# Transposes of a hybrid encoder block, written in pairs between its products

## The chip, the cores and the metric

The kernel runs on one core of a Trainium2 chip. The metric is device time in microseconds (us) for one launch. TensorE (PE in the profile) does the matrix products and the transposes; its weight loads are listed as PEld. VectorE is DVE, ScalarE is ACT, GpSimd is POOL, and SyncE is SP, which here only issues the loads of weights.

## The reference

One block of an encoder on x of 256 tokens by 2048 channels, in float32:

```python
proj = h @ w_in[l]
q, k, v, r, af, ab, hy_u, gate_logits = jnp.split(proj, split_idx, axis=-1)
y_gla = _gla_branch(q, k, v, r, af, ab, ...)   # 4 heads, chunks of 64 tokens, both directions
y_hy = _hyena_branch(hy_u, ...)                # short convolution, then z = gate * (conv(z) + skip*z), twice
g = jax.nn.sigmoid(gate_logits...).reshape(B, L, N_BRANCH, D)
merged = g[:, :, 0, :] * (y_gla @ w_gla_o[l]) + g[:, :, 1, :] * (y_hy @ w_hy_o[l])
mix = merged @ w_out[l]
h = _layernorm(DEEPNORM_ALPHA * h + mix, ln1_g[l], ln1_b[l])
ff = jnp.square(jax.nn.relu(h @ w_ff1[l])) @ w_ff2[l]
h = _layernorm(DEEPNORM_ALPHA * h + ff, ln2_g[l], ln2_b[l])
```

In the first branch each head's result o (256 x 512) is scaled by the reciprocal root of its mean square, by a learned gain and by a gate, which gives y. In the second branch the long convolutions are done as products with Fourier matrices.

## The kernel before

All weights lie in blocks of 128 x 2048 in the order of their use. `fetch` loads a block and splits each half into a high and a low part (`whi`, by ACT, L83; `wlo`, by DVE, L84), and `next_block` hands one out. Activations are held the same way in two parts. A product of two such numbers is three passes (high x low, high x high, low x high).

There are two kinds of product groups. `channel_pair` makes 128 channels by 256 tokens at a time; its `channel_products` has 16 high products of 512 columns (L144) and 16 low ones of 256 columns (L148) for each block. `token_group` makes 256 tokens by 512 channels; its `token_products` runs over the 16 slices of the contraction (kt) and the two halves of the tokens (tb), three products of 512 columns each (L196 to L198), and accumulates each half in one PSUM bank over four blocks.

Side work is put among these groups by hand. `later(d, fn)` files a function that is due d blocks on. After every block, `pump` calls what is due, and `drain` calls all that is left. This sets the order in which the program is written. The order in which each engine's instructions finally stand is made by a planner, which may move an instruction against its neighbours where its data and its priority allow it. `tc.keep_in_program_order(ins)` pins an instruction behind the one written before it on the same engine.

The side work that the change touches, in order of time:

- The heads (`gla_gates`, `gla_scores`, `gla_out`, filed 0, 4 and 7 blocks after each head's start, heads 6 blocks apart). `gla_gates` has products `z` (L504), then on ACT the gate pieces `ga` and `gm` (L508, L509), Exp and Ln (L511, L512), on DVE the running sums `gb`, then on ACT the exponentials `e` (L524, L525, L530) of each direction. `gla_scores` has products `s` (L580) and splits their result into `sth` and `stl`. `gla_out` has 12 products `o` (L296 to L298), ACT's square `y<-o` with its sum (L604), the small steps of the root (`rq_t`, `rq_y`, `rs`), DVE's `y` (L606), and 8 transposes of y into two banks `yt` (L613), which are split into yT.
- The convolution in 8 chunks of 256 channels. `hy_v` and `hy_x1` transpose the short convolution's results by `to_tokens` (`vt`, `x1t`, L673, 4 transposes each). `hy_fwd`, `hy_mul` and `hy_inv` make the long convolution. The second `hy_inv` has products `yp`, ACT's copy `zg` (L742), 4 transposes into `yT` (L746), and a product with x2, which goes to DRAM as `yd` and is read back as `yr` after the g2 groups.
- `merged`: for each of 4 groups, 8 transposes of the merged result into `mt` (L805), split into mT.
- The output product `wo` on mT, the first layer norm and the MLP. The pools `hp` and `qp` are closed and `ep` is opened ahead of wo.

A transpose is a TensorE instruction with the data as the moving operand's partner and `ident` as the other, 128 x 128 to PSUM.

Of the kernel before, what the change touches and what calls it, by code (L numbers as in the profile page):

```python
# [41 lines left out]
def block_kernel(  # L42
# [95 lines left out]
    def channel_products(ps, act, half, kts, ts=FULL, opens=True):  # L138
        hi, lo = half
        at = [(kt, slice(kt % 8 * P, (kt % 8 + 1) * P)) for kt in kts]  # L140

        def high():
            for kt, js in at:
                MM(ps[:, :, ts], hi[:, js], act[:, kt, :, ts], start=(kt == 0 and opens), stop=(kt == KT - 1))  # L144

        def low():
            for kt, js in at:
                MM(ps[:, 0, ts], lo[:, js], act[:, kt, 0, ts], start=False, stop=False)  # L148

        for part in (high, low) if kts[0] == 0 else (low, high):  # L150
            part()
# [33 lines left out]
    def token_products(pss, act, blocks, tbs, b0):  # L185
        for b, parts in enumerate(blocks):
            for h in range(2):
                hi, lo = parts[h]
                for j in range(2):
                    kt = (b0 + b) * 4 + h * 2 + j  # L190
                    wh = hi[:, j * 512:(j + 1) * 512]
                    wl = lo[:, j * 512:(j + 1) * 512]
                    for tb in tbs:
                        sh = act[:, kt, 0, tb * P:(tb + 1) * P]
                        sl = act[:, kt, 1, tb * P:(tb + 1) * P]
                        MM(pss[tb], sh, wh, start=(kt == 0), stop=False)  # L196
                        MM(pss[tb], sh, wl, start=False, stop=False)  # L197
                        MM(pss[tb], sl, wh, start=False, stop=(kt == KT - 1))  # L198

    def token_group(act, name):  # L200
        pss = [psum_main(f"{name}_{tb}") for tb in range(NT)]
# [390 lines left out]
    def gla_out(h):  # L592
        def run():
# [3 lines left out]
            for ib in range(NT):  # L597
                po = psum_side(f"o{h}{ib}")
                for jb in range(NT):
# [5 lines left out]
                hst["root"] = rsqrt_eps(rs, ss, 1.0 / 512.0, gp, f"rq{h}{ib}")  # L605
                nc.vector.scalar_tensor_tensor(  # L606
                    y[:, ib, :], po, rs, g_sb[:, ib, h * 512:(h + 1) * 512], op0=ALU.mult, op1=ALU.mult)
            for k2 in range(2):
                pt = psum_side(f"yt{h}{k2}")
                for kk in range(2):  # L610
                    for ib in range(NT):
                        kt = 2 * k2 + kk
                        nc.tensor.transpose(  # L613
                            pt[:, kk * L + ib * P:kk * L + (ib + 1) * P],
                            y[:, ib, kt * P:(kt + 1) * P], ident)
# [53 lines left out]
    def to_tokens(src, name):  # L669
        pt = psum_side(name)  # L670
        for c in range(2):
            for tb in range(NT):
                nc.tensor.transpose(pt[:, tb * CW + c * P:tb * CW + (c + 1) * P], src[:, c, tb * P:(tb + 1) * P], ident)  # L673
        return pt.rearrange("p (a b) -> p a b", a=2)

    def z_tiles(name):
        return (hp.tile([P, NT, CW], F32R, tag="zh", bufs=2, name=f"zh{name}"),
# [1 line left out]

    def hy_v(c):  # L680
        def run():
            z = z_tiles(f"{c}0")
            split_hi_lo(z[0], z[1], to_tokens(cst.pop(("v", c)), f"vt{c}"))
            cst[("z", c, 0)] = z
        return run

    def hy_x1(c):
        def run():
            x1 = hp.tile([P, NT, CW], F32, tag="x1", name=f"x1_{c}")
            nc.scalar.copy(x1, to_tokens(cst.pop(("x1c", c)), f"x1t{c}"))  # L690
            cst[("x1", c)] = x1
        return run

    def hy_fwd(c, o):
# [32 lines left out]
    def hy_inv(c, o):  # L727
        def run():
# [11 lines left out]
            else:  # L740
                zf = hp.tile([P, NT, CW], F32, tag="zf", name=f"zg{c}")
                nc.scalar.copy(zf, py3)  # L742
                pt = psum_side(f"yT{c}")
                for cc in range(2):
                    for tb in range(NT):
                        nc.tensor.transpose(pt[:, cc * L + tb * P:cc * L + (tb + 1) * P], zf[:, tb, cc * P:(cc + 1) * P], ident)  # L746
                yo = hp.tile([P, 2, L], F32, tag="zf", name=f"yo{c}")
                nc.vector.tensor_tensor(yo, pt.rearrange("p (a b) -> p a b", a=2), cst.pop(("x2", c)), op=ALU.mult)
                yd = drp.tile([P, 2, L], F32, tag=f"yd{c}", name=f"yd{c}")
                nc.gpsimd.dma_start(yd, yo)  # L750
                yh_dram[c] = yd
        return run

    go_done = [0]
# [26 lines left out]
            gla_o_group()  # L781


    g2_sb = qp.tile([P, 4, NT, 512], F32, tag="G", name="g2_sb")
# [5 lines left out]
    yhT = act_tile(base, "yT", "yh")  # L790
    for c in range(NCH):
        yr = hp.tile([P, 2, L], F32, tag="cv", bufs=2, name=f"yr{c}")
        nc.gpsimd.dma_start(yr, yh_dram[c])
        split_hi_lo(yhT[:, 2 * c:2 * c + 2, 0], yhT[:, 2 * c:2 * c + 2, 1], yr)
    mT = act_tile(base, "xT", "mT")

    def merged(g):
        def run():
            mg = m_group(g)
            for k2 in range(2):  # L800
                pt = psum_side(f"mt{g}{k2}")
                for kk in range(2):
                    for tb in range(NT):
                        kt = 2 * k2 + kk
                        nc.tensor.transpose(  # L805
                            pt[:, kk * L + tb * P:kk * L + (tb + 1) * P],
                            mg[:, tb, kt * P:(kt + 1) * P], ident)
# [12 lines left out]
    drain()  # L820
    hstk.close()
    qkg.close()


    ep = ctx.enter_context(tc.tile_pool(name="ep", bufs=1))
    zr = base.tile([P, 4, D], F32, tag="yT", name="zr")
    z1 = zr[:, 0:2]
    nc.scalar.dma_start(z1, x.rearrange("(a p) d -> p a d", p=P))

    def load_rows(i0):  # L830
        rows = zr[:, 2:4]
# [339 lines left out]
```

## Time and profile before

| | us |
|---|---|
| median of 3 runs | 1862.57 |
| lowest and highest | 1861.92, 1862.78 |
| the profiled execution | 1862.62 |
| its span in the profile | 1860.8 |

The profile is of one execution. Times on its rows count from the start of the span. A row of a group gives the engine, the line, the operation, the tiles (out<-in), the shapes and the count, then busy time and the mean duration. The waits view tells who waited for whom, with the total, the count and the longest. In the timeline a row starts with the start and the duration in us. A product's record is longer than its step, since products are pipelined: the step is the distance from one start to the next. Some records of products can be missing. A row of the windows view has the window, its length, busy time and instructions of PE, PEld, DVE, ACT and POOL, the granted clock of TensorE, the share of the DMA engines and GB/s.

### The profile page before, as it was taken

How to read it: one execution, taken by the hardware profiler on the slowest of the kernel's cores; microseconds unless marked ns; L12 is line 12 of the kernel's file. 1: busy time of each engine (PE TensorE's matmuls, PEld its weight loads, DVE VectorE, ACT ScalarE, POOL GpSimd, SP SyncE). 2: the span in 40 equal slices, each digit the busy share in tenths (PEclk: the TensorE clock that was granted, in tenths of full speed). 3: DMA queues.
4: the chain of work that ended last, by engine and by line, in shares of the span. 5: the costliest groups of instructions: out<-in, count | busy, mean ns of one | idle time of the engine just before them, and what ended most of it. 6: DMA issues, size and time to landing. Idle time of an engine off the chain costs nothing.

```text
span 1860.8 us, 23989 instructions
## 1 busy us (share of the span) xinstructions
PE 1852.2 (100%) x9471; PEld 1576.7 (85%) x9471; DVE 1286.1 (69%) x1628; ACT 934.5 (50%) x1268; POOL 30.8 (2%) x61
## 2 busy tenths in 40 slices
PE   9999999999999999999999999999999999999999
PEld 7888888888888888888888889888888888888887
DVE  6787878765788988888645567666555554665557
ACT  5555558765555555555444445444434443444332
POOL 1000000000000000000000000000000000000000
PEclk9999999999999999999999999999999999999999
DMA  7677664445555555566555764555545554545553
GB/s 286 235 251 263 243 233 168 157 159 195 191 199 193 195 217 190 203 218 222 197 188 193 277 219 156 194 209 192 193 186 199 183 197 186 201 184 188 196 192 125
DMA packets 59536, 375.51 MB, mean 202 GB/s; under 512 B 6720, under 2 KB 9184, under 8 KB 20000
## 3 DMA queue, kind: packets, MB, share of 16 engines
q1 hardware_dynamic: 46080, 324.03, 47.2%
q0 software_dynamic: 6288, 30.16, 4.4%
q10 hardware_dynamic: 7056, 19.80, 2.8%
q8 instruction: 74, 1.21, 0.3%
q14 instruction: 38, 0.31, 0.0%
HBM read 357.19 MB, written 16.78 MB: 201 GB/s over the span
## 4 chain that ended last, share of the span: by engine, by line
PE 98%; DVE 1%; DMA 0%; ACT 0%; issue 0%; SPq 0%; DVEq 0%
PE f L144 12%; PE f L148 7%; PE w L198 6%; PE w L197 6%; PE w L196 6%; PE uz L144 3%; PE uv L144 3%; PE ux L144 3%; PE g L196 3%; PE g L198 3%; PE g L197 3%; PE uv L148 2%; PE ux L148 2%; PE uz L148 2%; PE k L144 2%; PE r L196 2%
## 5 line engine op out<-in xcount | busy, mean ns | idle before, releaser
L84 DVE TENSOR_TENSOR wlo<-raw,whi 128x1024 fp32r<-128x1024 f32 x590 | 720.0, 1223 | 351.8 <-ACT whi L83 350.4
L83 ACT CAST whi<-raw 128x1024 fp32r<-128x1024 f32 x590 | 619.6, 1051 | 490.6 <-PE w L198 188.2
L144 PE MATMUL f<-hT,whi 128*128 128x512 f32 (+1 forms) x1048 | 246.4, 386 | 0.0
L144 PEld LDWEIGHTS f<-hT,whi 128*128 128x128 f32 x1048 | 190.1, 188 | 35.6
L197 PE MATMUL w<-wlo,f 128*128 128x512 f32 x480 | 186.7, 389 | 0.0
L198 PE MATMUL w<-whi,f 128*128 128x512 f32 x480 | 186.7, 389 | 0.0
L196 PE MATMUL w<-whi,f 128*128 128x512 f32 x480 | 167.4, 389 | 0.0
L148 PEld LDWEIGHTS f<-hT,wlo 128*128 128x128 f32 x1048 | 134.1, 191 | 4.8
L148 PE MATMUL f<-hT,wlo 128*128 128x256 f32 (+1 forms) x1048 | 135.8, 282 | 0.0
L156 ACT ACTIVATE f_l<-f 128x256 f32<-128x256 f32 x64 | 24.5, 384 | 163.8 <-PE f L144 163.8
L197 PEld LDWEIGHTS w<-wlo,f 128*128 128x128 f32 x480 | 90.1, 188 | 18.7
L196 PEld LDWEIGHTS w<-whi,f 128*128 128x128 f32 x480 | 90.1, 188 | 18.7
L198 PEld LDWEIGHTS w<-whi,f 128*128 128x128 f32 x480 | 90.1, 188 | 18.7
L157 DVE SCALAR_TENSOR_TENSOR f_s<-f,f_l 128x256 f32<-128x256 f32 x64 | 27.2, 425 | 107.1 <-ACT f_l L156 107.1
L197 PE MATMUL g<-wlo,xT 128*128 128x512 f32 x256 | 99.9, 390 | 0.0
L198 PE MATMUL g<-whi,xT 128*128 128x512 f32 x256 | 99.8, 390 | 0.0
L196 PE MATMUL g<-whi,xT 128*128 128x512 f32 x256 | 92.6, 390 | 0.0
L144 PE MATMUL uz<-xT,whi 128*128 128x512 f32 x256 | 63.7, 393 | 0.0
L144 PE MATMUL ux<-xT,whi 128*128 128x512 f32 x256 | 63.6, 391 | 0.0
L144 PE MATMUL uv<-xT,whi 128*128 128x512 f32 x256 | 63.1, 391 | 0.0
L198 PEld LDWEIGHTS g<-whi,xT 128*128 128x128 f32 x256 | 48.1, 188 | 9.9
L197 PEld LDWEIGHTS g<-wlo,xT 128*128 128x128 f32 x256 | 48.1, 188 | 9.8
(399 smaller groups left out, 3189.1 us busy)
## 6 DMA issues: line engine op xcount, KB each, us to landing
raw<-wblk SPq DMA_DIRECT2D x302, 1024.0 KB, 4.8
Td<-T POOLq DMA_DIRECT2D x16, 768.0 KB, 4.0
Tl<-Td POOLq DMA_DIRECT2D x16, 768.0 KB, 4.6
w<-w4s ACTq DMA_DIRECT2D x16, 512.0 KB, 5.2
xw<-first SPq DMA_DIRECT2D x7, 640.0 KB, 10.3
zr<-ln_rows ACTq DMA_DIRECT2D x4, 1024.0 KB, 10.0
dec<-decay_in ACTq DMA_DIRECT2D x8, 256.0 KB, 4.7
yd<-yo POOLq DMA_DIRECT2D x8, 256.0 KB, 3.5
```

The source lines that it names most:

```text
L83: nc.scalar.copy(hi, src)
L84: nc.vector.tensor_tensor(lo, src, hi.bitcast(F32), op=ALU.subtract)
L144: MM(ps[:, :, ts], hi[:, js], act[:, kt, :, ts], start=(kt == 0 and opens), stop=(kt == KT - 1))
L148: MM(ps[:, 0, ts], lo[:, js], act[:, kt, 0, ts], start=False, stop=False)
L156: nc.scalar.activation(low, ps[:, 1], AF.Copy, scale=scale)
L157: nc.vector.scalar_tensor_tensor(dst, ps[:, 0], scale, low, op0=ALU.mult, op1=ALU.add)
L196: MM(pss[tb], sh, wh, start=(kt == 0), stop=False)
L197: MM(pss[tb], sh, wl, start=False, stop=False)
L198: MM(pss[tb], sl, wh, start=False, stop=(kt == KT - 1))
```

## The change

There is a second queue of side work, `drips`. Each entry writes two transposes (one column tile for the two halves of the tokens), and the entry's bank is split or copied when its last pair is written. `drip` takes one entry. `channel_products` calls it after every second high product (not after the eighth of a half), `token_products` after every three products. The transposes of an entry are pinned in program order by `hold`, and `MMh` pins the first product after them. `rest` empties the queue, at the start of every `pump` and in `drain`.

The heads' transposes go through `by_pairs`, one block later than before; those of `hy_v`, `hy_x1` and the merged groups go through the queue too; those of the convolution's result go in after three empty entries. The last chunk of the convolution is split straight into yhT, without the way through DRAM, and the other seven are read back one by one during the g2 groups. The x rows are loaded, and the first output group `wo0` is written, ahead of the closing and opening of pools.

```diff
+    drips = deque()
+    held = [False]
+    def hold(ins):
+        tc.keep_in_program_order(ins)
+    def drip():
+        if drips:
+            held[0] = bool(drips.popleft()())
+    def MMh(*a, **k):
+        ins = MM(*a, **k)
+        if held[0]:
+            held[0] = False
+            hold(ins)
+        return ins
+    def rest():
+        while drips:
+            drip()
     def pump():
+        rest()
...
     def drain():
+        rest()
         for e in sorted(side, key=lambda e: e[:2]):
             e[2]()
+            rest()
         side.clear()
+    def by_pairs(name, src, done):
+        for k2 in range(2):
+            box = []
+            for kk in range(2):
+                def pair(k2=k2, kk=kk, box=box):
+                    if not box:
+                        box.append(psum_side(f"{name}{k2}"))
+                    kt = 2 * k2 + kk
+                    for tb in range(NT):
+                        hold(nc.tensor.transpose(box[0][:, kk * L + tb * P:kk * L + (tb + 1) * P],
+                                                 src[:, tb, kt * P:(kt + 1) * P], ident))
+                    if kk == 1:
+                        done(k2, box[0])
+                    return True
+                drips.append(pair)
...
-                MM(ps[:, :, ts], hi[:, js], act[:, kt, :, ts], start=(kt == 0 and opens), stop=(kt == KT - 1))
+                MMh(ps[:, :, ts], hi[:, js], act[:, kt, :, ts], start=(kt == 0 and opens), stop=(kt == KT - 1))
+                if ts == FULL and kt % 2 == 1 and kt % 8 < 7:
+                    drip()
...
-                        MM(pss[tb], sh, wh, start=(kt == 0), stop=False)
+                        MMh(pss[tb], sh, wh, start=(kt == 0), stop=False)
                         MM(pss[tb], sh, wl, start=False, stop=False)
                         MM(pss[tb], sl, wh, start=False, stop=(kt == KT - 1))
+                        drip()
...
-            for k2 in range(2):
-                pt = psum_side(f"yt{h}{k2}")
...
+            def turned(k2, pt):
                 s = slice(4 * h + 2 * k2, 4 * h + 2 * k2 + 2)
                 split_hi_lo(yT[:, s, 0], yT[:, s, 1], pt.rearrange("p (a b) -> p a b", a=2))
+            later(1, lambda: by_pairs(f"yt{h}", y, turned))
...
-                pt = psum_side(f"yT{c}")
+                box = []
+                def pair(cc):
...
+                        if c == NCH - 1:
+                            split_hi_lo(yhT[:, 2 * c:, 0], yhT[:, 2 * c:, 1], yo)
+                            return True
...
+                drips.extend([lambda: None] * 3)
                 for cc in range(2):
+                    drips.append(lambda cc=cc: pair(cc))
...
+    yhT = act_tile(base, "yT", "yh")
+    def reload(c):
...
+    for c in range(NCH - 1):
+        later(c, reload(c))
     g2_sb = qp.tile([P, 4, NT, 512], F32, tag="G", name="g2_sb")
...
-            mg = m_group(g)
...
+            by_pairs(f"mt{g}", m_group(g), turned)
...
+    zr = base.tile([P, 4, D], F32, tag="yT", name="zr")
+    z1 = zr[:, 0:2]
+    nc.scalar.dma_start(z1, x.rearrange("(a p) d -> p a d", p=P))
+    wo0 = token_group(mT, "wo0")
     drain()
     hstk.close()
     qkg.close()
...
-        pss = token_group(mT, f"wo{g}")
+        pss = token_group(mT, f"wo{g}") if g else wo0
```

More of the change, by code (lines that the diff above doesn't have):

```diff
@@ L667, in short_conv, with to_tokens, pair @@
         return y
-    def to_tokens(src, name):
-        pt = psum_side(name)
+    def to_tokens(src, name, done):
+        box = []
         for c in range(2):
-            for tb in range(NT):
-                nc.tensor.transpose(pt[:, tb * CW + c * P:tb * CW + (c + 1) * P], src[:, c, tb * P:(tb + 1) * P], ident)
-        return pt.rearrange("p (a b) -> p a b", a=2)
+            def pair(c=c):
+                if c == 0:
+                    box.append(psum_side(name))
+                for tb in range(NT):
+                    hold(nc.tensor.transpose(box[0][:, tb * CW + c * P:tb * CW + (c + 1) * P],
+                                             src[:, c, tb * P:(tb + 1) * P], ident))
+                if c == 1:
+                    done(box[0].rearrange("p (a b) -> p a b", a=2))
+                return True
+            drips.append(pair)
     def z_tiles(name):
@@ L688, in run, with done @@
         def run():
-            x1 = hp.tile([P, NT, CW], F32, tag="x1", name=f"x1_{c}")
-            nc.scalar.copy(x1, to_tokens(cst.pop(("x1c", c)), f"x1t{c}"))
-            cst[("x1", c)] = x1
+            def done(pt):
+                x1 = hp.tile([P, NT, CW], F32, tag="x1", name=f"x1_{c}")
+                nc.scalar.copy(x1, pt)
+                cst[("x1", c)] = x1
+            to_tokens(cst.pop(("x1c", c)), f"x1t{c}", done)
         return run
@@ L781, in block_kernel, with run @@
             gla_o_group()
+    yhT = act_tile(base, "yT", "yh")
+    def reload(c):
+        def run():
+            yr = hp.tile([P, 2, L], F32, tag="cv", bufs=2, name=f"yr{c}")
+            nc.gpsimd.dma_start(yr, yh_dram[c])
+            split_hi_lo(yhT[:, 2 * c:2 * c + 2, 0], yhT[:, 2 * c:2 * c + 2, 1], yr)
+        return run
+    for c in range(NCH - 1):
+        later(c, reload(c))
     g2_sb = qp.tile([P, 4, NT, 512], F32, tag="G", name="g2_sb")
@@ L789, in block_kernel @@
     drain()
[L790 to L794, printed above, removed]
     mT = act_tile(base, "xT", "mT")
@@ L798, in run, with turned @@
         def run():
-            mg = m_group(g)
[L800 to L807, printed above, removed]
+            def turned(k2, pt):
                 s = slice(4 * g + 2 * k2, 4 * g + 2 * k2 + 2)
                 split_hi_lo(mT[:, s, 0], mT[:, s, 1], pt.rearrange("p (a b) -> p a b", a=2))
+            by_pairs(f"mt{g}", m_group(g), turned)
         return run
```

39 lines of the change are left out of this document (20 added, 19 removed).

## The prediction

> **What bounds the kernel now.** I read the page first, then the waits of PE, then the timeline around the transposes that move.
>
> ```profile
> span 1860.8 us, 23989 instructions
> PE 1852.2 (100%) x9471; PEld 1576.7 (85%) x9471; DVE 1286.1 (69%) x1628; ACT 934.5 (50%) x1268; POOL 30.8 (2%) x61
> PE 98%; DVE 1%; DMA 0%; ACT 0%; issue 0%; SPq 0%; DVEq 0%
> PE warm L260 <- DVE ones_sb L293: 1.5, 1, 1.5
> PE mlp L329 <- issue: 1.5, 1, 1.5
> ```
>
> Nearly the whole chain is PE behind PE, and PE's listed waits (the two longest are shown; two more are under 1 us each) all lie in the first 27 us. The time is therefore the length of one instruction stream. A change can shorten it only by making PE's instructions cheaper, and lengthens it by every wait that PE then meets. ACT and DVE have room on average, but between 300 and 430 us they work through long queues for the heads, and the change makes PE depend on those queues. The profiled execution took 1862.62 us around its span of 1860.8; the median of the runs is 1862.57, so the sum below starts from 1862.6.
>
> **Price of a transpose, in a run and in a pair.** No transpose is added or removed: 32 each for the heads, the values, the x1 gate, the result of the convolution and the merged groups, 160 in all. Only their grouping changes: as the built program has them, 80 pairs, where the trace shows 36 runs. One run in this trace already is a pair between products:
>
> ```profile
> 429.45 0.39 PE L198 MATMUL g<-whi,xT 128*128 128x512 f32 x1
> 429.68 0.39 PE L196 MATMUL g<-whi,xT 128*128 128x512 f32 x1
> 429.91 0.38 PE L613 MATMUL yt<-ident,y 128*128 128x128 f32 x2
> 430.05 0.48 PE L197 MATMUL g<-wlo,xT 128*128 128x512 f32 x1
> 430.37 0.40 PE L198 MATMUL g<-whi,xT 128*128 128x512 f32 x1
> 430.60 0.82 PE L613 MATMUL yt<-ident,y 128*128 128x128 f32 x6
> 431.18 0.48 PE L196 MATMUL g<-whi,xT 128*128 128x512 f32 x1
> 431.49 0.39 PE L197 MATMUL g<-wlo,xT 128*128 128x512 f32 x1
> ```
>
> A product's step is 0.23 (429.45 to 429.68). From 429.68 to 430.37 are two products and the pair: 0.69 - 0.46 = 0.23, or 0.115 a transpose. From 430.37 to 431.49 are two products and six: 1.12 - 0.46 = 0.66, or 0.11 a transpose. The fixed price of starting a run is thus about 0.01, and 44 more runs cost 0.4 us. Between ends of 0 and 0.03 a run this is 0 to 1.3; I take 0.5.
>
> **The heads: a wait that did not exist.** Before, nothing tied a head's transposes to a place; the planner let them fall where y was long ready. After, each pair is pinned behind the product written before it, and the next product behind the pair. A product accumulates into the bank of its predecessor, so everything later in that token group waits too. In the built order of before 73, 49, 50 and 31 products stand between the last `o` of heads 0 to 3 and their first transpose; in that of the changed program 0, 27, 27 and 27. I work out head 0 on the clock of the trace, whose order is still the same there.
>
> ```profile
> 304.08 0.72 PE L504 MATMUL z<-as_sb,ws 128*128 128x256 f32 x4
> 304.63 0.40 PE L197 MATMUL v<-wlo,xT 128*128 128x512 f32 x1
> ...
> 312.37 0.39 PE L296 MATMUL o<-yg,sth 128*128 128x512 f32 x1
> ...
> 315.18 0.63 PE L196 MATMUL v<-whi,xT 128*128 128x512 f32 x2
> ```
> ```profile
> 304.68 0.49 ACT L508 ACTIVATE ga<-z,ba_sb 128x256 f32<-128x256 f32 x1
> ...
> 307.54 0.69 ACT L492 CAST ws<-wr 128x512 fp32r<-128x512 f32 x1
> 308.05 0.70 ACT L83 CAST sth<-st 128x512 fp32r<-128x512 f32 x1
> 308.57 0.71 ACT L511 ACTIVATE ga<-ga 128x512 f32<-128x512 f32 x1
> 309.10 1.11 ACT L83 CAST whi<-raw 128x1024 fp32r<-128x1024 f32 x1
> 310.04 0.71 ACT L511 ACTIVATE ga<-ga 128x512 f32<-128x512 f32 x1
> 310.57 0.78 ACT L512 ACTIVATE ga<-ga,ones_sb 128x512 f32<-128x512 f32 x1
> 313.68 0.69 ACT L524 ACTIVATE e<-gb 128x512 f32<-128x512 f32 x1
> 316.17 0.63 ACT L604 ACTIVATE y<-o 128x512 f32<-128x512 f32 x1
> 316.74 0.64 ACT L604 ACTIVATE y<-o 128x512 f32<-128x512 f32 x1
> ```
> ```profile
> 314.42 0.69 DVE L513 SCALAR_TENSOR_TENSOR gm<-ga,gm 128x512 f32<-128x512 f32 x1
> 316.76 1.26 DVE L520 TENSOR_TENSOR_SCAN gb<-scan_sb,gm 128x256 f32<-128x256 f32 x2
> 324.63 1.23 DVE L84 TENSOR_TENSOR wlo<-raw,whi 128x1024 fp32r<-128x1024 f32 x1
> 326.15 1.41 DVE L606 SCALAR_TENSOR_TENSOR y<-o,rs,g_sb 128x512 f32<-128x512 f32 x2
> ```
>
> Head 0. PE leaves `z` at 304.6 and has 2 products (0.45) where 34 stood before. The `o` products need `sth`, whose place in ACT's order is unchanged: it ends at 308.75. First wait: 308.75 - 305.05 = 3.7. The 12 `o` products take 2.8 (312.37 to 315.18), to 311.55. Meanwhile ACT goes on with the next head's gates: two Exp and two Ln at steps of 0.55; the first Ln ends at about 310.4. DVE then does both `gm` and the first two scans, 0.6 + 0.6 + 1.26 with starts overlapping, to 312.9. ACT's exponentials of one direction take 2.5 (313.68 to 316.17), one y square 0.57 (316.17 to 316.74), the other direction 2.5 and the second square 0.57: 319.2. Four small root steps on ACT and six on DVE at 0.1 to 0.2 add about 1.5, the two writes of y 1.4: 322.1. Second wait: 322.1 - 311.55 = 10.5. Head 0 costs 14.2.
>
> Heads 1 and 2. From `z` to the first pair PE has 0.5 of `z`, 24 + 10 + 27 products and 12 `o`, that is 73 x 0.227 = 16.6, so 17.1. ACT's order over the same stretch for head 1 is: 0.7 until it reaches the gates, eight gate pieces 2.86 (304.68 to 307.54), `ws` 0.5, two Exp and two Ln 2.3, two splits of v 1.0, five casts of weights 4.7 (0.94 each, 309.10 to 310.04), two direction sets 5.0, two squares 1.1, small ones 1.0: 19.2. DVE then has part of one weight subtraction and the whole of another (1.23 each) among the small steps, and y: 3.8. The wait is 23.0 - 17.1 = 5.9; I take 6.0. Head 2 has in that stretch no `ws` (0.5), no splits of v (1.0) and one cast fewer (0.94), but a copy of g (0.5) and 0.6 of waiting for the scan: ACT 17.9, DVE 4.0, and 21.9 - 17.1 = 4.8. Head 3 has no next head's gates in its queue, so that the shortest chain (below) fits behind its 27 products: 0. Nothing in the trace shows these waits themselves. From below they are bounded by the shortest chain (a square, the small steps, two writes: 4 us) against 0 and 27 products (6.1): 4 us in all. From above they are bounded by the trace's own distance from `o` to y, 315.2 to 327.6, 12.4: 3.7 + 12.4 + 2 x 6.3 = 28.7. The orders built are known, and the casts that lengthen the trace's chain are counted one by one, so I take 25.0, near the upper end.
>
> **The convolution's result.** `yT` reads `zg`, ACT's copy of `yp`. The three empty drips delay the pair in the writing, but the planner put `yp` late, and in four of the eight chunks (22 products stand between in the other four) the pair follows the last `yp` directly.
>
> ```profile
> L742 ACT COPY zg<-yp x8: 587/587/590, 551.7 to 904.1; 128x512 f32<-128x512 f32 x8
> 429.00 0.39 PE L196 MATMUL g<-whi,xT 128*128 128x512 f32 x1
> ```
>
> PE waits for a product's end after its last step (0.39 - 0.23 = 0.16) and the copy (0.59), with some 0.06 for the signals: 0.8 x 4 = 3.2. If ACT is in a cast when `yp` ends, up to 1.0 more each; if products slip between, 0. The values and the x1 gate read what was ready a block earlier: 0.
>
> **The clock after a wait.**
>
> ```profile
> 24.76:28.17 3.41, 1.98 (x8) 1.45 (x9) 1.62 (x3) 2.27 (x3) 0.00 (x0) 1.00 0.92 375
> 28.17:31.58 3.41, 3.41 (x15) 3.11 (x14) 3.35 (x8) 2.93 (x6) 0.00 (x0) 0.50 0.30 71
> ```
>
> After a stretch with PE busy for 1.98 of 3.41 us (third number) the granted clock (third from the end) was 0.50 for the next 3.41, which lost 1.7 of PE's work. Three waits (10.5, 6.0, 4.8) are far longer than that idle part. I charge each with one such stretch, 5.1 in all, between 0.85 and 2.5 each for where the stretch begins. The first wait of head 0 costs nothing more: ACT's queue, not `o`, sets the second.
>
> The Trainium skill ("TensorE: Matmul & The Clock Gate", Part 1) asks for a whole idle window of about 3.4 us before it halves the clock; this trace halved it after one that was idle for less than half, and the measurement decides. By the page's rule the 4.8 would meet such a window in fewer than half of its positions and the 6.0 in three of four, and the loss would be about 3.7 instead of 5.1.
>
> **Edits that cost nothing.** The reload of seven chunks during the g2 groups keeps its places in POOL's order, POOL is busy for 30.8 us of the span, and the last chunk loses its two DMAs; the cover is the g2 groups, of which PE has none waiting. If it were gone, one reload of some 4 us would show. Writing wo0 ahead of the pools' change moves the loads of x and of the rows and the table load within ACT's order; PE has no wait there now, so there is none to remove, and the last merged transposes already fell between wo products. 0, at most 1.3 for the table load.
>
> **The sum.** 0.5 + 14.2 + 6.0 + 4.8 + 3.2 + 5.1 = 33.8; 1862.6 + 33.8 = 1896.4, forecast 1896. Its own range: without loss of clock and with the waits 5 us shorter 1886, with 2.5 each for the clock and the copies late 1903.
>
> **Rivals.** (1) The pairs hide their weight loads behind the long products. A 128-column transpose would then step by half of a 256-column product:
>
> ```profile
> 1158.26 1.91 PE f L148 x16
> ```
>
> 1.91 / 16 / 2 = 0.06 instead of 0.11, 160 times: 8 us gained, 1888. Against it stands the pair at 429.91, which paid 0.115. The Trainium skill (same page, Part 2, "Back-to-back issue gap") gives about 81 ns for a 128-column step in a stream; by that the gain would be 4.5. Chance 4%.
>
> (2) Only head 0 waits, because ACT reaches the squares of heads 1 and 2 before the casts: 1862.6 + 0.5 + 14.2 + 1.7 + 3.2 = 1882. For it: a chain of 4 us would fit behind 27 products. Against it: the direction sets stand ahead of the second square in ACT's order. Chance 6%.
>
> (3) Not slower: the held order never makes PE wait, because y is written when PE arrives. Place: the first pair of heads 0, 1 and 2; price 0; it decides when the chain from `o` to y is under 6.1 us for heads 1 and 2 and under nothing at all for head 0. Then the pairs cost 0.5 and the time is 1863. The trace's 12.4 for that chain speaks against it, and so does the `mlp` wait of 1.5, during which no later product passed. A form of it in which the moved work also gains something gives 1858. Chance 4%, half of it within 0.2%.
>
> (4) After each wait the clock stays half for two or three stretches, because the groups that follow are broken by pairs and small products: 2 to 4 more for each of three, 1905. For it: nothing in the trace shows a recovery after 10 us of idling. Chance 8%.
>
> My forecast has the remaining 78%. The range from 1885 to 1904 takes in the forecast's bounds and most of (1); it leaves out (2), (3) and part of (4). A measurement of this kernel tells 0.2%, or 3.7 us, from no change. Faster gets 0.02, the same 0.02, slower 0.96.
>
> **What would show it right or wrong.** In the profile after, PE's waits should list `yt` behind DVE's y for some 21 us in three or four places, `o` behind ACT's `sth` for 3.7, and `yT` behind `zg` at four times 0.8; the granted clock should be 0.5 for some 3.4 us after each head's wait; a transpose should still step by 0.11. I am wrong if PE shows no wait between 300 and 430 us, if the wait for `yt` lies under 10 us in all, or if the stretch from 440 us on is more than 8 us shorter or longer than before.

## The result, and the profile after

| | us |
|---|---|
| before, beside the changed kernel | 1862.24 (1861.70 to 1862.78, 4 runs) |
| after | 1893.94 (1893.15 to 1896.83, 4 runs) |
| ratio after to before | 1.0178, 95% interval 1.0166 to 1.0190 |
| the profiled execution after, its span | 1893.15, 1891.3 |

The change costs 31.7 us. The head of the page, the chain by engine, and PE's waits (us in total, times, longest) of the changed kernel:

```profile
span 1891.3 us, 23988 instructions
PE 1859.3 (98%) x9471; PEld 1575.3 (83%) x9471; DVE 1287.7 (68%) x1628; ACT 935.3 (49%) x1268; POOL 29.8 (2%) x59
PE 84%; issue 10%; DVE 3%; ACT 2%; DMA 1%; POOL 0%; SPq 0%; DVEq 0%; POOLq 0%; ACTq 0%
```
```profile
PE yt L163 <- DVE y L650: 13.6, 5, 8.4
PE yt L163 <- DVE rq_t L262: 4.7, 1, 4.7
PE o L340 <- ACT sth L83: 3.5, 1, 3.5
PE yT L801 <- ACT zg L793: 2.7, 4, 0.7
```

The same 9471 PE instructions take 30.5 us more span. Four entries are new, 24.5 us together, all of them PE at a pinned pair, or at `o`, which now comes early. PE's busy time rises by 7.1 as well, with the same instructions: most of it is products at a lower granted clock (0.50 in four places of the heads), below.

Where the time went is read best in the windows view, with windows that start at the same instruction in both kernels: the first `z` of head 0, the first `uv`, `ho`, `wo` and `f`. Before, then after (window, its length, busy of PE, PEld, DVE, ACT, POOL, clock, DMA share, GB/s):

```profile
279.73:461.89 182.16, 182.16 (x920) 152.39 (x919) 126.18 (x216) 126.25 (x252) 0.53 (x1) 1.00 0.45 168
461.89:958.36 496.47, 496.47 (x2593) 425.89 (x2592) 404.47 (x465) 264.69 (x353) 16.63 (x31) 1.00 0.55 202
958.36:1048.08 89.72, 89.72 (x409) 74.56 (x408) 49.94 (x51) 37.44 (x40) 0.00 (x0) 1.00 0.51 188
```
```profile
276.72:488.60 211.88, 190.07 (x920) 156.09 (x919) 127.89 (x216) 126.94 (x252) 0.54 (x1) 0.95 0.41 144
488.60:988.69 500.09, 497.39 (x2594) 424.17 (x2593) 404.03 (x465) 264.68 (x353) 15.61 (x29) 1.00 0.56 200
988.69:1078.55 89.86, 89.86 (x410) 74.17 (x409) 50.22 (x51) 37.55 (x40) 0.00 (x0) 1.00 0.53 187
```

The heads cost 29.7 us, the convolution 3.6, the merged groups 0.1, all the rest under 0.1. The sum is 33.5. The span rose by only 30.5 because the first `z` came 3.0 us earlier in this execution; that is the opening, in front of anything that the change touches. In the 14 profiles of this study the first `z` started anywhere from 276.4 to 280.5 us. The length of a stage does not carry that spread, so the experiments are read by stages beside their times.

Inside the heads, the timeline at the first wait, and the end of `o` and the first pair of heads 0 and 1:

```profile
300.85 0.72 PE L548 MATMUL z<-as_sb,ws 128*128 128x256 f32 x4
...
301.63 0.40 PE L241 MATMUL v<-whi,xT 128*128 128x512 f32 x1
305.57 0.79 PE L340 MATMUL o<-yg,sth 128*128 128x512 f32 x1 [3.54 <-ACT sth L83]
...
309.58 0.40 PE L342 MATMUL o<-yg,stl 128*128 128x512 f32 x1
318.40 0.47 PE L163 MATMUL yt<-ident,y 128*128 128x128 f32 x1 [8.43 <-DVE y L650]
319.06 0.47 PE L163 MATMUL yt<-ident,y 128*128 128x128 f32 x1 [0.19 <-DVE y L650]
```
```profile
360.97 0.39 PE L241 MATMUL v<-whi,xT 128*128 128x512 f32 x1
366.05 0.33 PE L163 MATMUL yt<-ident,y 128*128 128x128 f32 x1 [4.70 <-DVE rq_t L262]
367.09 0.48 PE L163 MATMUL yt<-ident,y 128*128 128x128 f32 x1 [0.71 <-DVE y L650]
367.22 0.77 PE L128 MATMUL v<-whi,xT 128*128 128x512 f32 x1
```

The second number of a row is the record, not the step; a wait is the distance of two starts less the step (0.23 for a product, 0.11 for a transpose). So 305.57 - 301.63 is a wait of 3.7, 318.40 - 309.58 one of 8.6, and the second transpose, whose operand is the second half of y, adds 0.55. Head 1 waits 4.9 + 0.9, head 2 by the same reading 4.1 + 0.55, head 3 not at all. In the convolution the pairs of four of the eight chunks wait 0.84 each (the row of `yT` above).

### The profile page after: what moved, and what is told of

It is laid out like the page before. It is cut to its first block, busy times and chain, and to the rows that moved or that the text cites. A ratio compares the mean times of both kernels' runs of the same rounds, so it can differ in the third digit from the quotient of the medians.

```text
span 1891.3 us, 23988 instructions
## 1 busy us (share of the span) xinstructions
PE 1859.3 (98%) x9471; PEld 1575.3 (83%) x9471; DVE 1287.7 (68%) x1628; ACT 935.3 (49%) x1268; POOL 29.8 (2%) x59
## 4 chain that ended last, share of the span: by engine, by line
PE 84%; issue 10%; DVE 3%; ACT 2%; DMA 1%; POOL 0%; SPq 0%; DVEq 0%; POOLq 0%; ACTq 0%
PE f L128 12%; PE f L191 6%; PE w L241 6%; PE w L240 6%; PE w L128 6%; PE uz L128 3%; PE uv L128 3%; PE ux L128 3%; PE g L241 3%; PE g L240 3%; PE g L128 3%; PE uv L191 2%; PE ux L191 2%; PE uz L191 2%; PE go L128 2%
## 5 line engine op out<-in xcount | busy, mean ns | idle before, releaser
L128 PE MATMUL uz<-xT,whi 128*128 128x512 f32 x256 | 68.5, 400 | 0.0
L241 PEld LDWEIGHTS g<-whi,xT 128*128 128x128 f32 x256 | 48.4, 189 | 10.2
L128 PEld LDWEIGHTS g<-whi,xT 128*128 128x128 f32 x256 | 48.4, 189 | 9.6
```

Source lines behind the costliest of these rows:

```text
L128: ins = MM(*a, **k)
```

## The experiments

"Stage" is the length from the first `z` to the first `uv` (heads; before 182.2, after 211.9) or from there to the first `ho` (convolution; before 496.5, after 500.1).

**The heads' transposes as before, in the changed kernel.**

```diff
-            later(1, lambda: by_pairs(f"yt{h}", y, turned))
+            for k2 in range(2):
+                pt = psum_side(f"yt{h}{k2}")
+                ...                       # 4 plain transposes, split, as before
```

> The changed kernel, with the heads' 8 transposes written in one go inside gla_out as in the kernel before, unpinned; everything else as changed. Theory (the time goes where PE stands at the heads' pinned transposes, and in the half clock behind it): no wait between 300 and 430 us, the clock 1.00 there, the four yT waits of 0.84 stay and the other pairs cost some 0.5: 1862.2 + 3.4 + 0.5 = 1866.1 us. Rival A (pairs as such are dear, wherever they stand): 16 of 80 pairs are gone, so about a fifth of the 31.7 us, which leaves 1887.5. Rival B (the early loads and the early output group cost part of it): some us more than 1866.

Measured: 1866.22 us (1862.53 to 1867.70), ratio 1.0023 [1.0014, 1.0031]. The heads' stage is 182.2, as before; the convolution's is 500.1, as after; no stretch from 30 us to the last 2 us has the clock below 1.00. The heads' pairs carry all but some 4 us.

**The heads' pairs alone, in the kernel before.** The queue of drips, `by_pairs` and the calls of `drip` are added to the kernel before, and only the heads use them.

> The kernel before, with the heads' transposes alone changed to pinned pairs one block later; the convolution, the merged result, the reload and the output group as before. Theory: it takes over the whole of the heads' loss and none of the rest: 1893.9 - 3.4 - 0.5 = 1890.0 us, with waits of 3.9, 9.4, 6.1 and 5.0 us less a step each, and half clock behind each. Rival A (the pairs as such): 16 of 80 pairs, 1868.5. Rival B (the heads wait only because the other moved work crowds ACT and DVE at that place): under 1880.

Measured: 1893.20 us (1892.13 to 1895.32), ratio 1.0171 [1.0158, 1.0185]. The heads' stage is 214.1, the convolution's 496.5. So the heads alone bring the loss, and nothing else of the change is needed for it. It is 3 us more than the theory gave, although the waits are the same but for head 0's first for y, which is 0.85 shorter. The windows show why; here head 1's wait (365.85 to 370.94) in this kernel:

```profile
365.81:369.22 3.41, 0.43 (x2) 0.01 (x1) 3.34 (x10) 2.30 (x7) 0.00 (x0) 1.00 0.00 0
369.22:372.63 3.41, 1.12 (x3) 0.79 (x4) 2.64 (x7) 0.00 (x0) 0.00 (x0) 0.50 0.79 298
372.63:376.05 3.42, 3.42 (x11) 2.62 (x10) 0.69 (x1) 0.59 (x1) 0.00 (x0) 0.50 0.03 12
376.05:379.46 3.41, 3.41 (x17) 2.74 (x16) 1.62 (x2) 1.53 (x2) 0.00 (x0) 1.00 0.02 5
```

and in the changed kernel:

```profile
359.74:363.15 3.41, 1.61 (x8) 1.00 (x6) 3.38 (x11) 3.41 (x11) 0.00 (x0) 1.00 0.00 0
363.15:366.56 3.41, 0.33 (x1) 0.14 (x1) 3.31 (x10) 0.08 (x1) 0.00 (x0) 1.00 0.58 159
366.56:369.97 3.41, 2.88 (x9) 2.29 (x10) 0.52 (x2) 0.59 (x1) 0.00 (x0) 0.50 0.36 151
369.97:373.39 3.42, 3.42 (x18) 2.78 (x17) 1.64 (x2) 1.53 (x2) 0.00 (x0) 1.00 0.02 5
```

In all 14 profiles the granted clock stays at one value for whole multiples of 3.41 us between 30 and 1840 us, and it does not change where a wait begins or ends: it changes on a grid of its own. The same wait fell on it so that one half stretch followed in one execution, and two in the other (11 products are recorded in a busy stretch at half clock, 17 or 18 in one at full clock). One stretch more is some 1.7 us a head. In the whole stage of the heads PE was busy for 20.7 us at half clock here, and for 12.9 in the changed kernel.

**The same pairs, pinned, four blocks on.**

```diff
-            later(1, lambda: by_pairs(f"yt{h}", y, turned))
+            later(4, lambda: by_pairs(f"yt{h}", y, turned))
```

> The changed kernel with one number changed: the heads' pairs are filed four blocks on instead of one. All pairs stay pinned. In the built order 71, 119, 119 and 99 products now stand between the last o and the first yt (0, 27, 27, 27 before this edit), and 34, 12 and 24 between z and o. Theory (it is the distance, not the pin, that makes PE wait): no wait at the heads, 1866.1 us as for the kernel with the heads as before, with 8 more pairs' price within 0.2. Rival A (a pinned pair costs by itself): about 1894. Rival B (a pinned pair always meets some queue on ACT or DVE, so the waits only shrink): 1875 to 1885.

Measured: 1867.06 us (1864.60 to 1869.59), ratio 1.0026 [1.0016, 1.0037]. The heads' stage is 183.4, and PE's waits hold no `yt` and no `o`. In the profile the first pairs start 15.6, 26.5, 27.0 and 22.7 us after the start of the last `o`, and the second half of y is done at 13.2, 15.9, 13.6 and 3.6. A pin makes no wait where the operand is ready; rivals A and B are out. The stage is 1.2 longer than with the plain transposes. A pair's rows account for about 0.2 of it (16 pairs at 0.0125 over the run of 8); the planner also placed the score products otherwise, and that part was not settled.

**Two blocks on.**

```diff
-            later(1, lambda: by_pairs(f"yt{h}", y, turned))
+            later(2, lambda: by_pairs(f"yt{h}", y, turned))
```

> The changed kernel with the heads' pairs filed two blocks on instead of one. In the built order 25, 24 and 24 products stand between z and o, and 0, 53, 51 and 51 between o and yt. In the profile after, y of heads 1 and 2 was ready 27 x 0.227 + 5.1 = 11.2 and 6.1 + 4.3 = 10.4 us after the last o. Theory (the wait is that chain less the products in between): 53 and 51 products are 12.0 and 11.6 us, so heads 1 and 2 wait no longer; 25 products (5.7) cover sth (3.9); head 0, with 0 products, still waits some 9.3 + 0.6 and loses 1.7 to 3.4 to the clock: 1867 + 9.9 + 2.5 = 1879 us. Rival A (the chain is slowed by whatever PE does in the meantime, so the waits only shrink): two more waits of 1 to 3 us, 1882 to 1885. Rival B (the pins cost, not the distance): 1893.

Measured: 1880.96 us (1879.61 to 1882.93), ratio 1.0103 [1.0090, 1.0117]; the heads' stage is 197.3.

```profile
PE yt L163 <- DVE y L650: 10.3, 3, 9.1
...
PE g L240 <- DVE wlo L84: 0.8, 2, 0.4
PE g L128 <- ACT whi L83: 0.5, 1, 0.5
```

Head 0, with no product in between, waits 9.2 + 0.55, as theory had it; the wait for `sth` is gone; the waits of 5.8 and 4.6 at heads 1 and 2 have shrunk to pieces of about 0.5 to 1.2, some of them for weights, 2.8 us in all. So rival A is there too, in a small size: the chain itself grew. The second half of y was done 14.7 and 13.7 us after the start of the last `o` of heads 1 and 2, where it was 12.2 and 11.1 in the changed kernel. Distance in products decides, and it has to be compared with the chain behind the operand as it is in the new order.

**No pins at all.**

```diff
     def hold(ins):
-        tc.keep_in_program_order(ins)
+        return ins
```

> The changed kernel with hold emptied: transposes are written in pairs at the same places, but nothing is pinned. In the built order the planner gathers them again (73, 73, 50 and 31 products between o and yt as before, 22 between yp and yT in all eight chunks). Theory: 1862.2 to 1862.7 us, so the early output group, the early loads and the seven reloads are worth nothing in either direction. Rival A (they cost): up to 1866. Rival B (they gain, and the waits hid the gain): 1858 to 1861.

Measured: 1861.10 us (1858.79 to 1862.03) beside 1861.96 before, ratio 0.9996 [0.9987, 1.0005]; stages 182.2 and 496.4. The reloads and the early output group bring no gain and no loss that shows. The planner gathers most of the transposes again (47 runs in the profile, where there were 36 before and 80 in the changed kernel), so this run says little of the price of pairs.

**PE kept busy while it waits.**

```diff
+                def filled():
+                    pt = psum_side(f"fill{h}")
+                    for _ in range((41, 27, 22, 0)[h]):
+                        hold(MM(pt, xT[:, 0, 0, 0:P], ..., start=True, stop=True))
+                    return first_pair()
```

> The changed kernel with products that nobody uses (128 x 512, xT by xT into a spare bank) written ahead of the first pair of heads 0, 1 and 2: 41, 27 and 22 of them, at 0.227 each 9.3, 6.1 and 5.0 us, as long as PE stood there. The planner puts 16 of head 0's between its o products. The waits stay covered, none is taken away; only PE's idling goes. Theory (idle PE loses the clock afterwards): the half stretches at 312 to 322, at 367 and at 414 go, the one behind the wait for sth at 305 stays; 1893.9 - 1.9 - 1.7 - 1.7 = 1888.6 us, up to 2 more if the products at half clock near 305 overrun. Rival A (the half clock costs nothing that counts, since ACT and DVE set the pace there): 1894. Rival B (the added products push the chain itself out): over 1895.

Measured: 1892.15 us (1890.00 to 1893.14), ratio 1.0164 [1.0150, 1.0178]; the heads' stage 208.7, that is 3.2 less than after; span 1888.2 against 1891.3, with the first `z` at the same place within 0.1.

```profile
306.01:309.42 3.41, 3.41 (x10) 2.64 (x9) 2.64 (x5) 1.86 (x4) 0.00 (x0) 0.50 0.28 82
309.42:312.84 3.42, 3.42 (x16) 2.82 (x15) 3.42 (x9) 3.02 (x10) 0.00 (x0) 1.00 0.00 0
...
364.40:367.80 3.40, 3.40 (x18) 2.79 (x17) 1.70 (x5) 0.01 (x1) 0.00 (x0) 1.00 0.69 277
```

One half stretch is left, the one behind `sth`. There are 90 products more, and the stage is shorter: they take 20.4 us where 19.6 of waiting stood, so the clock had cost some 3.2 + 0.8 = 4.0 us behind the three waits. The expected 5.3 was too much, and the median, with the opening's spread in it, lies between theory and rival A; the ratio's interval overlaps that of the changed kernel, so the stage alone shows the theory's direction.

**What sets y for heads 1 and 2.** Two edits, one for each queue, and both together:

```diff
-                for c in range(2):
-                    for i in ((0, 1, 2) if d == 0 else (1, 2, 3)):
-                        ...               # six exponentials of 64 columns into e3
+                nc.scalar.activation(e3, b, AF.Exp)
```

> The changed kernel with each head's six exponentials of 64 columns for each direction (one group, step 1.43 us for the six in the profile after) replaced by one of 512 columns (step 0.52), which leaves out the offset of each chunk. ACT's queue ahead of the second square and the root steps is so 0.9 to 1.8 us shorter for heads 0, 1 and 2; the built order of PE is unchanged. Theory as the prediction counted it (ACT's queue is a sum, and all that stands in it ahead of y delays y): each of the three waits 1.8 shorter, 1893.9 - 5.4 = 1888.5 us. Rival A (the weights' splits in that queue wait for buffers that PE frees only when it reaches the pair, so the queue's length does not count for heads 1 and 2): head 0 alone gains, 1892.2, and the waits of 5.1 + 1.0 and 4.3 + 0.66 stay. Rival B (DVE sets y): no change, 1894.

Measured: 1894.36 us (1892.50 to 1895.75), ratio 1.0176 [1.0163, 1.0190]. From the first `z` of head 1's gates to head 0's first pair it takes 16.0 us (303.60 to 319.63) where the changed kernel took 17.6 (300.85 to 318.40). But heads 1 and 2 first wait 4.8 and 4.0, where it was 4.9 and 4.1, and only head 1's second wait is shorter (0.55 for 0.9). At head 1 ACT was done earlier and idled instead:

```profile
358.51 0.53 ACT L258 ACTIVATE rq_t<-ss,eps_sb 128x1 f32<-128x1 f32 x2
359.63 0.63 ACT L568 ACTIVATE e<-gb 128x512 f32<-128x512 f32 x1 [0.59 <-DVE gb L564]
```

So the length of ACT's queue does not set these two waits. Nor do weights that wait for their buffers (rival A's reason): the casts in that stretch start without idle. What remains is DVE, which in the changed kernel's rows works without a gap of 0.1 us from 355.5 to y at 365.3:

```profile
355.47 1.22 DVE L84 TENSOR_TENSOR wlo<-raw,whi 128x1024 fp32r<-128x1024 f32 x1
356.67 1.26 DVE L564 TENSOR_TENSOR_SCAN gb<-scan_sb,gm 128x256 f32<-128x256 f32 x2
...
362.45 1.22 DVE L84 TENSOR_TENSOR wlo<-raw,whi 128x1024 fp32r<-128x1024 f32 x1
363.58 0.21 DVE L261 SCALAR_TENSOR_TENSOR rq_t<-rq_y,rq_v 128x1 f32<-128x1 f32 x1
363.91 1.22 DVE L84 TENSOR_TENSOR wlo<-raw,whi 128x1024 fp32r<-128x1024 f32 x1
365.05 0.15 DVE L263 TENSOR_TENSOR rs<-rq_y,rq_t 128x1 f32<-128x1 f32 x1
365.25 0.75 DVE L650 SCALAR_TENSOR_TENSOR y<-o,rs,g_sb 128x512 f32<-128x512 f32 x1
```

From the scans to y DVE takes 8.6 us here (356.67 to 365.25) and 8.6 with the short exponentials (358.33 to 366.89). The two subtractions of weights that stand ahead of y had their casts done at 361.5 and 363.1, so they waited for DVE's own order. The gain at head 0 does not show in the time: the stage is 211.1 for 211.9, because in this execution each of the four waits brought two half stretches or more, and PE was busy for 19.1 us at half clock where it was 12.9.

```diff
+                GT = nc.gpsimd.tensor_tensor
-                TT(ka, ...); TT(kx[...], ...); TT(qx[...], ...)
+                GT(ka, ...); GT(kx[...], ...); GT(qx[...], ...)
```

> The changed kernel with five of each direction's eight products of the gates (ka, the two kx and the DVE half of qx, 128 x 128 to 128 x 256) issued on GpSimd instead of DVE: by the profile after 0.33 + 3 x 0.20 = 0.93 us off DVE's queue for each direction, 1.9 for each head, in the stretch ahead of y; ACT's queue is as it was. Theory (the run with shorter exponentials left the waits of heads 1 and 2 at 5.1 and 4.2, and DVE was busy without a gap from 356.7 us to y there, so DVE's queue sets them): the waits of heads 1 and 2 shrink by 1 to 1.9 each, until ACT's casts and root steps, due about a microsecond earlier, set them; head 0, which ACT sets, stays. About 1891. Rival A (both queues end together, or GpSimd slows DVE): under 0.7 shorter, 1893 to 1894.

The edit moves four of each direction's seven products on DVE, not five of eight; the 0.93 us is the sum for four.

Measured: 1897.44 us (1896.13 to 1899.01), ratio 1.0191 [1.0177, 1.0205], with waits of 5.1 + 0.9 and 4.1 + 0.55, no shorter. The interval overlaps that of the changed kernel. The stage is 2.65 us longer, and the clock accounts for it: two half stretches followed heads 1 and 2, so that PE was busy at half clock for 19.1 us where it was 12.9, and half of the difference is 3.1. A part of rival A is what happened. DVE's rows from 300 to 440 us, changed kernel first, then this one (count, busy, mean ns):

```profile
L577 DVE TENSOR_TENSOR qi<-q_sb,e 128x512 f32<-128x512 f32 x6 | 4.1, 677 | 0.2 <-ACT e L568 0.2
L564 DVE TENSOR_TENSOR_SCAN gb<-scan_sb,gm 128x256 f32<-128x256 f32 x6 | 3.8, 670 | 0.0
L586 DVE TENSOR_TENSOR kk<-k_sb,e 128x256 f32<-128x256 f32 x6 | 2.5, 418 | 0.0
```
```profile
L564 DVE TENSOR_TENSOR_SCAN gb<-scan_sb,gm 128x256 f32<-128x256 f32 x6 | 4.9, 858 | 0.0
L577 DVE TENSOR_TENSOR qi<-q_sb,e 128x512 f32<-128x512 f32 x6 | 4.8, 796 | 0.4 <-ACT e L568 0.4
L587 DVE TENSOR_TENSOR kk<-k_sb,e 128x256 f32<-128x256 f32 x6 | 3.8, 628 | 0.0
```

DVE has fewer instructions, and these three, some of which run beside GpSimd, take 18 to 50% longer on average (418 to 628 ns for `kk`). From the scans to y of head 1 DVE took 8.7 us (358.58 to 367.32), four products a direction fewer notwithstanding: the relief was paid back in the same queue. ACT's casts ended within 0.1 us of the two last subtractions here, so this run alone does not say which of the two queues set y. The Trainium skill ("GPSIMD Engine Reference", section 1) lists the SBUF interfaces of this engine as shared with VectorE, with contention for DVE instructions that have two SBUF inputs; the three rows are of that kind, and the trace agrees.

> Both edits together: the gates' five products on GpSimd (DVE 1.9 us shorter for each head) and one exponential of 512 columns for six of 64 (ACT 1.8 shorter), which leaves out the offset of each chunk. Theory (heads 1 and 2 wait for whichever of two queues ends last, of about equal length): the waits of heads 1 and 2, 5.1 and 4.2, shrink by 1.5 to 1.9 each, more than the sum of what either edit did alone; head 0's by 1.5 as with the exponentials alone. Some 1889 where the clock loses one stretch for each wait. Rival A (neither queue, but the weights' buffers that PE frees): the waits of heads 1 and 2 stay at 5.1 and 4.2, 1892 to 1894.

Measured, with both edits: 1894.94 us (1893.40 to 1898.44), ratio 1.0180 [1.0166, 1.0194]; the waits of heads 1 and 2 are 5.3 + 0.55 and 1.4 + 3.9. Together they are no shorter. By its wording rival A stands, but not by its reason: the casts ended 0.75 and 1.3 us ahead of the two last subtractions of head 1, and DVE was again slowed by GpSimd and took 8.9 us from the scans to y (359.02 to 367.94). That DVE's queue sets heads 1 and 2 is therefore read from the rows and from ACT's idling; no run has shown it by taking work off DVE.

**The output group back behind the pools' change,** on the kernel with the heads four blocks on (1867.1 us):

```diff
-    wo0 = token_group(mT, "wo0")
     drain()
     ...
-        pss = token_group(mT, f"wo{g}") if g else wo0
+        pss = token_group(mT, f"wo{g}")
```

> The kernel with the heads' pairs four blocks on (1867.1 us), with the first output group and the loads of x put back behind the pools' change, as in the kernel before. Theory from the built order (the early group is what the last merged group's pinned pairs are written between; without it they follow the last ho product directly and wait for DVE's sums of the merged result): two new waits of 1.6 and 0.5 us, 1869.2. Rival A (as the prediction had it, the early group is worth nothing): 1867.1. Rival B (the early group costs something by the moved loads): below 1866.

Measured: 1869.73 us (1867.38 to 1870.53), ratio 1.0042 [1.0030, 1.0055] against 1.0026 without this edit.

```profile
PE mt L163 <- DVE k_sb L883: 1.8, 2, 1.6
```

The stage from the first `ho` to the first `wo` is 92.8 for 89.9, and a half stretch follows (1054.78 to 1058.19) and takes 0.8 of the next stage. So the early group is worth some 3 us, but only with the merged pairs pinned (without pins it brought no gain that shows): it is the cover for a wait that the pins would make.

**More empty entries for the convolution,** on the same kernel:

```diff
-                drips.extend([lambda: None] * 3)
+                drips.extend([lambda: None] * 6)
```

> The kernel with the heads' pairs four blocks on (1867.1 us), with six empty entries instead of three ahead of the convolution's pairs. In the built order at least 19 products then stand between yp and yT in all eight chunks (0 in four of them with three). Theory A (distance alone decides): the four yT waits of 0.84 go and nothing comes, 1863.7. Theory B (from the built order: in four chunks the second pair then lands directly ahead of the next chunk's yp products, which need a bank that DVE frees only after reading that pair): the wait moves from yT to yp and is longer, four times 1.9, so 1867.1 - 3.4 + 7.5 = 1871.

Measured: 1871.58 us (1870.28 to 1874.77), ratio 1.0062 [1.0048, 1.0075]; the convolution's stage is 504.7.

```profile
PE yp L340 <- DVE Yl L84: 7.2, 4, 1.8
```

This is theory B in place and size: the wait for `zg` is gone and four longer ones have come, 2.0 each from start to start less a step. Its reason was off: `yp`, now directly behind the pair, waits for `Yl`, DVE's split of its own operand, and for no bank.

**The convolution's pairs not pinned,** on the same kernel:

```diff
-                        hold(nc.tensor.transpose(pt[...], zf[...], ident))
+                        nc.tensor.transpose(pt[...], zf[...], ident)
...
-                    return True
+                    return False
```

> The kernel with the heads' pairs four blocks on, and the convolution's pairs written at the same places but not pinned (in the built order 2 or 22 products between yp and yT). All other pairs stay pinned. Theory (no pin with a late operand is left): the four waits of 0.84 shrink to 0.4 or less, and what remains above the kernel before is the pairs' own price: 1863 to 1864.5 us, no faster than the kernel before (1861.9). Rival A (the pairs gain something that the waits hid): below 1860. Rival B (the pins of the values, the x1 gate and the merged groups cost too): 1867, as with them pinned.

Measured: 1864.74 us (1862.55 to 1868.33), ratio 1.0016 [1.0007, 1.0025]; stages 183.4 and 497.7, three waits of 0.39. This is the fastest version with pinned pairs. It still does not reach the kernel before, and no version here is faster than that kernel beyond the interval of its ratio.

## Why the prediction was right, and where its steps were not

- **The bound and the kind of loss.** Right: PE's stream was the time, and each wait at a pin lengthened it. Shown by the heads' pairs alone (1.0171), by their absence (1.0023) and by distance (1.0026 with the pins kept).
- **Head 0.** 14.2 forecast; measured 3.7 for `sth`, 1.5 because `o` itself ran partly at half clock (its 12 products took from 305.57 to 309.8, 4.2 for 2.8), 8.6 + 0.55 for y: 14.3 in all. The term "second wait: 10.5" was 1.35 too large, and "the first wait of head 0 costs nothing more" held, for one reason: not `o` but the queue behind it set y's end, so that the 1.5 lost at `o` came off the wait for y. With the short exponentials in ACT's queue it came some 1.5 earlier, which bears that out. The second transpose started 18.2 us behind the first `z` (300.85 to 319.06); the sum had y done at 18.0 (304.08 to 322.1).
- **Heads 1 and 2.** 6.0 and 4.8 forecast, 5.8 and 4.6 measured, head 3 none. But the step "ACT's order over the same stretch ... 19.2" failed as a mechanism: 1.8 us less in ACT's queue did not shorten them. The sum hit the number by way of the wrong queue, and that was luck: DVE's queue beside it, which the prediction only counted from ACT's end on, was as long by its rows. (One count was off, too: 73 products, and not 49, stand between the last `o` of head 1 and its first transpose in the profile before. No term rests on it.)
- **The clock.** 5.1 forecast. Products behind the three waits lost some 4.6 in the profile after (3.0, 2.8 and 3.4 us at half), and keeping PE busy gave back 4.0. The mechanism is shown. The size depends on how the wait lies on the grid. Behind head 0 the clock was half for 10.24 us, but most of that lay within the wait; with two stretches behind each of the other waits, as in the kernel with the heads' pairs alone, the heads' stage is 2.2 longer. So the two stretches of rival (4) occur, as a part of the spread, but its reason is not borne out: every busy stretch at half clock (85% and more) was followed by one at full clock, whether pairs broke it or not.
- **The convolution.** 3.2 forecast, 4 x 0.84 = 3.4 measured, in four chunks of eight.
- **The price of a pair.** Right: 0.115 a transpose; outside the heads the pairs cost 0.5 at most beside their waits, by the stages. Rival (1), 8 us gained, is out; so are (2) and (3), since heads 1 and 2 waited.
- **Edits at nothing.** The reload: right (no pins at all, 0.9996). For the output group the step "PE has no wait there now, so there is none to remove" asked about the kernel before only. With pinned merged pairs and the group behind the pools' change there is one, some 3 us with its clock.
- **The sum.** 33.8 forecast, 33.5 by stages. The medians differ by 31.7, and the forecast of 1896 lies 2.1 above the median of 1893.94. The opening, 3.0 us shorter in the profile after, is of that size; the prediction had taken it for fixed. That the sum agrees with the stages to 0.3 us is luck in part, since one of its queues was the wrong one.

## What to carry to other kernels

Before pinning an instruction on the engine that bounds the kernel, count the work that stands ahead of it and compare it with the chain that makes its operand: 27 products (6.1 us) were too few for a chain of 10 to 11 us, and 15.6 us and more left no wait. Count the chain in the new order, since it can grow (from 12.2 to 14.7 us two blocks on). An instruction that a planner leaves late may be late for that reason: in the kernel before, the first half of y of heads 0 and 1 was done 12.0 and 13.2 us after the last `o` began, and the transposes stood at 16.8. And compare stages that start at the same instruction, not spans: an opening that varies by 4 us hides or feigns an effect of 2.

## What the runs showed of the hardware

- **When the clock halves.** Take every stretch of the 3.41 us grid in all 14 traces, from 30 to 1840 us, by the share of it in which PE's records show work. At full clock all 22 stretches with 42% or less were followed by one at half, of the 13 between 47 and 75% one was, and with 80% and more none was. At half clock all 18 stretches with 79% or less were followed by another half one, and all 23 with 85% or more by one at full clock. Four waits of 2.0 us did not halve it in the run with more empty entries, where busy shares were 47% and more; one of 1.7 + 0.4 at the merged pairs did, at 48%. The Trainium skill ("TensorE: Matmul & The Clock Gate", Part 1) puts the change at a whole idle window; in these traces a window idle for 58% or more by the records always did, and the measurement decides. The stretch of the opening that the prediction had read (58%, then half) lies ahead of these 30 us and in the range in which only one of 13 was; why it halved the clock stays open. That the windows run freely, as the same section says, agrees with the one or two stretches behind equal waits.
- **DVE beside GpSimd.** Moving DVE work to an engine that was idle made three groups of instructions with two operands in SBUF 18 to 50% longer on average. `y`, which at head 1 came after GpSimd's last product, stayed at 744 ns for 746.
- **Transposes and the clock.** Runs of 2 to 8 transposes of 128 columns at 0.11 us each, 0.9 us at most, never lowered the granted clock as long as their operands were ready. By the shares above, so short a run would not lower it even if it counted as idle, so this does not tell how the clock counts transposes.
